# A score product on half of the array's rows becomes one on all 128, padded with zeros

## The chip, the cores and the metric

The kernel runs on one core of a Trainium2 chip. A core has a matrix engine (PE, with its weight loads shown apart as PEld), a vector engine (DVE), a scalar engine (ACT), a general engine (POOL) and queues that start transfers (SP). The metric is the time of one execution on the device, in microseconds (us); lower is better.

## The reference, cut to what matters

The program is one inference step of a backbone of two layers on 640 tokens: 128 of a prompt and 512 of an image. Each layer has a convolution, a gated recurrence and a differential attention side by side, then a feed-forward part. The change touches the attention alone:

```python
def one_block(qblk):                       # 128 queries
    s = einsum('bqhcd,bkhcd->bhcqk', qblk, k) * scale   # 4 heads, 2 maps c, 64 channels d
    p = softmax(s, axis=-1)
    w = p[:, :, 0] - lam * p[:, :, 1]
    return einsum('bhqk,bkhe->bqhe', w, v)
```

A head has 128 channels: 64 for its first map of scores and 64 for its second. The prompt attends to itself (128 keys). The 512 image queries attend to 640 keys: 128 of a cache and their own 512. Everything is float32.

## The kernel before, in words

**Exact products in parts.** The matrix engine gets its operands in a rounded 32-bit form (fp32r). A float32 factor is therefore kept as a high part and a low part, and a product is made of three: high by high, high by low, low by high. Nearly all large products of the kernel (L268 with channels on partitions, L279 with tokens on partitions) run over these three with all 128 rows, and an output takes 24 matmuls.

**Scores.** Since a map has only 64 channels, the parts share the 128 rows. `split_keys` (L948 to L955) makes, for each map `c` of a head, 128 rows of keys: the 64 rows of the map itself (`own`) hold the high parts, the 64 others (`other`) the low parts. `split_queries` (L957 to L964) makes three blocks of 128 columns for a tile of 128 queries: block 0 has the high parts of map 0 on both halves of the rows, block 1 those of map 1, and block 2 the low parts, map 0 on rows 0 to 63 and map 1 on rows 64 to 127. In `scores` (L973 to L1003) L987 multiplies block `c` by all 128 rows of keys, which gives high by high and high by low at once; L988 adds low by high, and takes only the 64 rows `rs` of the map:

```python
T.matmul(ps[:, hf, :320], lhsT=qs[n][:, c], rhs=ks[:, sl], start=True, stop=False)
T.matmul(ps[:, hf, :320], lhsT=qs[n][rs, 2], rhs=ks[rs, sl], start=False, stop=True)
```

This pair runs for two maps and for two halves of 320 keys, so a tile of queries takes eight matmuls, in turn on 128 and on 64 rows. There are four image tiles for each of four heads in two layers: 32 such tiles. A fifth tile of each head, the prompt's (L991), is made directly in float32 on 64 rows.

**A tile's way.** Behind the scores DVE takes the maximum over the keys (L994) and scales it (L995), and ACT makes the exponentials (L997). `weigh` (L1005) joins the two maps on DVE (L1007 to L1010), `turn` (L1013) transposes the weights on PE (L1016) and ACT copies them (L1017), `values` (L1020) multiplies them by the values (L1024). The weights of a tile are made one tile behind its scores. Two pairs of PSUM banks hold the scores of the two maps, so the next tile's scores need the exponentials of this one.

**What runs beside it.** `weave` puts one step of a list of large products behind each `yield` of the attention: products for gates (L268) beside heads 0 and 1 and the start of the recurrence (L279, then L268) beside heads 2 and 3. Their weights are split as they arrive by ACT (L249) and DVE (L250). `behind(last, taps, 4)` (L1002) puts four taps of the convolution (L639, DVE) behind the scaled maxima of each tile. The order on each engine is fixed when the program is built, by a planner that goes by priorities, dependencies and its own estimates of time; in the trace the first queries are split (L961 to L963) long before their scores.

**Storage.** `parts` (L1220) is a region of 3840 columns, taken anew in each layer. It holds the keys of two heads (2 times 1536 columns) and the queries of two tiles (2 times 384).

Of the kernel before, what the change touches and what calls it, by code (L numbers as in the profile page):

```python
# [15 lines left out]
ALU = mybir.AluOpType  # L16
AX = mybir.AxisListType

P = 128
# [5 lines left out]
# taps of the convolution beside the making of queries and keys, and beside a tile of scores  # L25
# [4 lines left out]
# columns of the parameter pack  # L30
# [5 lines left out]
# columns of the row pack (one layer)  # L36
# [3 lines left out]
class Arena:  # L40
    """Columns of one tile, given out and taken back in program order; the tile's
    own tracking orders the accesses. The part that has been free longest goes first."""
# [51 lines left out]
def tile_trunk_step(  # L94
# [33 lines left out]
    # ---------------------------------------------------------------- storage  # L128
# [41 lines left out]
    def banks(kind):  # L170
        """Banks for the large products; pairs for scores and levels; the rest."""
# [26 lines left out]
    # ---------------------------------------------------------------- helpers  # L198
# [12 lines left out]
    def flat(pair):  # L211
        """The first 640 columns of two banks."""
        return pair.rearrange("p b n -> p (b n)")[:, :NT]

    def f32(ap):
        return ap.bitcast(F32)
# [8 lines left out]
    def next_t():  # L225
        """For what is done with at once."""
        ctr["t"] += 1
        return ur[:, 3 + ctr["t"] % 2]

    def load_raw(src, n, at=None):  # L230
        """One panel of weights: n columns per partition."""
        if at is None:
            ctr["raw"] += 1
            at = rawt[:, ctr["raw"] % 2, :n]
        dst = at
        if len(src.shape) == 3:
            dst = at.rearrange("p (a b) -> p a b", a=src.shape[1])
        with hp():
            nc.sync.dma_start(dst, src)
        return at  # L240

    def split_cols(raw3):
        """Weights [128, K, c] into two parts that float32r holds exactly; list over k of (hi, lo)."""
# [16 lines left out]
    def gemm(wk, ak, hf):  # L260
        """sum_k w_k^T a_k for one half of the tokens; the three products that float32 holds."""
# [9 lines left out]
    def gemm_tm(wk, ak, i):  # L271
        """(token tile i of a)^T w; [128, 256]."""
# [9 lines left out]
    def panel8(src):  # L282
        """A panel [128, 8, 256]: two column tiles, each a list over k."""
        raw = load_raw(src, RAW).rearrange("p (k c) -> p k c", k=KD)
        return [split_cols(raw[:, :, c * P : (c + 1) * P]) for c in range(2)]
# [5 lines left out]
    def panel_wide(src, K):  # L291
        """A panel [128, K <= 4, 512]: four column tiles."""
# [8 lines left out]
    def rsqrt(dst, var, n):  # L301
        """dst = var ** -0.5 for var > 0."""
# [9 lines left out]
    def stat_rstd(s, sl, scale, eps, post=None, ring=None):  # L312
        """s: [128 ch, 640] whose column sums are the squares; 1 / rms of the tokens of sl
        on every partition, in a psum bank."""
# [15 lines left out]
    def streams(sl):  # L330
        """The parts of a slice of tokens that belong to the prompt (0) and to the latents (1)."""
# [6 lines left out]
    # ---------------------------------------------------------------- constants  # L338
# [16 lines left out]
    # ---------------------------------------------------------------- modulation  # L355
    def modulation(l, v, stage=None):
        """Vector v of the six of layer l: 1024 channels, both streams; channels on partitions.
        In steps of one panel."""
# [23 lines left out]
    def mod_finish(l, v, j=0, n=8):  # L382
        """n of the 8 tiles of channels of a vector, from j."""
# [10 lines left out]
    def mod_vectors(*regs):  # L394
        """The other vectors, the last of layer 0 first, on the vector engine, channels on
        partitions; in steps of one tile of channels."""
# [26 lines left out]
    def weave(core, fill, late=iter(())):  # L423
        """The steps of core with a step of fill behind each; the rest of fill before its end,
        with late."""
# [7 lines left out]
    def spread(fill, other):  # L433
        """The steps of fill, with one of other behind every third."""
# [9 lines left out]
    # ---------------------------------------------------------------- norm + modulation of the stream  # L444
# [19 lines left out]
    def make_h(xs, sq, l, which, hf):  # L464
        """h = rmsnorm(x) * (1 + scale) + shift, in two parts, for one half of the tokens."""
# [16 lines left out]
    # ---------------------------------------------------------------- layer parameters  # L482
    def layer_params(l):
        """Small vectors of a layer; 0 = -lambda, 1 = hgrn gain / 4, 2 = subln gain * (1 - lam_init),
        4..7 conv_b * 2, 8..11 ln_g / 2, 12..15 ln_b / 2."""
# [17 lines left out]
    def rope_tables(l):  # L503
        """Rotation tables with the gains in them: y = n * C + swap(n) * S."""
# [24 lines left out]
    def lower_bounds():  # L529
# [12 lines left out]
        for l in range(DEPTH):  # L542
            # rows: 0 = (1 - lb) / 2, 1 = lb + (1 - lb) / 2, 2 = -(1 - lb) / 2
# [10 lines left out]
    # ---------------------------------------------------------------- evictions  # L554
# [7 lines left out]
    def ev_silu2(dst):  # L562
        """2 silu(x) = (tanh(x / 2) + 1) x"""
# [8 lines left out]
    def tiles_g(jobs, lead=False):  # L572
        """jobs: (load, ((evict, k-list of activations), ...)); load() gives the column tiles of a
        panel. lead: the first two panels by halves, so that the second half may come later.
        In steps of half a column tile."""
# [21 lines left out]
    # ---------------------------------------------------------------- conv branch  # L597
# [32 lines left out]
    def conv_taps(l, pads, accs):  # L630
        """In steps of one tap."""
# [10 lines left out]
    def behind(ins, gen, n):  # L642
        """n steps of gen, not before ins on the vector engine."""
# [3 lines left out]
    def conv_norm(l, reg, accs):  # L647
        """Layer norm over 512 channels, in place; the accumulators hold twice the convolution.
        In steps of a few instructions."""
# [11 lines left out]
        for j in range(4):  # L661
            # in place: the prompt first, then the latents move down over the gap
# [15 lines left out]
    def conv_swish(l, reg, accs, out):  # L678
        """In steps of one tile."""
# [14 lines left out]
    # ---------------------------------------------------------------- HGRN  # L694
    def hgrn_v(l, out):
        """Values, tokens on partitions; [128, 5, 128] per head."""
# [10 lines left out]
    def hgrn_gemm(l, hb, h):  # L707
        """Queries (q), forget gates (f, b) and output gates (g) of a head; the last go to DRAM."""
# [10 lines left out]
    def both(rs, B=None):  # L719
        """Two regions as one, [128, 2, n]; with B: [128, blocks, 2, B], the first halves of the  # L720
        blocks of 2B from the first region and the second halves from the second."""
# [9 lines left out]
    def hgrn_core(l, h, vs, hb, bo):  # L731
        """Both directions of one head (b = backward, f = forward). q, k: [128 d, 2, 640]; chunks
        of 128 tokens, merged pairwise: at block length B the pairs (t, s) in the two halves of a
        block of 2B have the decay split at the middle, so that every factor is at most one. The
        first halves of the keys count forward and those of the queries backward, so one product
        holds both directions."""
# [63 lines left out]
        # states at chunk boundaries  # L800
# [57 lines left out]
    def token_norm(ot, scale, eps):  # L858
        """ot: [128 tok, 5, 128] in place / rms over the last axis."""
# [10 lines left out]
    # ---------------------------------------------------------------- attention  # L870
# [6 lines left out]
    def attn_qk(l, p, w, tabs):  # L877
        """Queries (w = 0) or keys (w = 1) of heads 2p, 2p+1: normed, rotated, transposed."""
# [18 lines left out]
        # prompt: gain only; latent: gain and rotation  # L897
# [23 lines left out]
    def attn_tr(l, p, w, reg, prep):  # L921
        """The queries or keys of attn_qk with the channels on partitions."""
        sq, s3, _ = prep
        # keys: 128 of the cache, 512 latents, 128 of the prompt; queries without the cache
# [22 lines left out]
    def split_keys(regs, parts, g):  # L947
        """Keys of head g on 128 rows for each of its two maps: (hi, lo) and (lo, hi)."""  # L948
        k = attn_views(regs[g // 2])[1][:, g % 2]
        ks = parts[:, g % 2 * 1536 : (g % 2 + 1) * 1536].rearrange("p (c t) -> p c t", c=2)  # L950
# [6 lines left out]
    def split_queries(q, dst):  # L957
        """A tile of queries as (hi, hi) of the first map, of the second, and (lo, lo) of both."""
        for c in range(2):
# [3 lines left out]
            V.tensor_tensor(out=dst[own, 2], in0=q[own], in1=f32(dst[own, c]), op=ALU.subtract)  # L963
        return dst  # L964

    def attn_core(l, p, regs, parts, keys, out, taps, ends):
        """Two heads; the weights of a tile of 128 queries are made one tile behind the scores.
        keys: the parts of the keys by head, made one head ahead; ends: what is left to do for
        the head before, and then for the last."""
# [5 lines left out]
        def scores(n, hh, i):  # L975
# [4 lines left out]
            for c in range(2):  # L980
                ps = wring.next()
                rs = slice(64 * c, 64 * (c + 1))
                if i:
                    ks = keys[2 * p + hh][:, c]
                    for hf in range(2):
                        sl = slice(hf * 320, (hf + 1) * 320)
                        T.matmul(ps[:, hf, :320], lhsT=qs[n][:, c], rhs=ks[:, sl], start=True, stop=False)  # L987
                        T.matmul(ps[:, hf, :320], lhsT=qs[n][rs, 2], rhs=ks[rs, sl], start=False, stop=True)  # L988
# [15 lines left out]
        def weigh(es, sm, nk):  # L1004
            # w' = e0 - lambda * (s0 / s1) * e1;  the weights are w' / s0  # L1005
# [37 lines left out]
        for n, it in enumerate(items + [None]):  # L1043
# [4 lines left out]
            if n + 1 < len(items) and items[n + 1][1]:  # L1048
                hh, i = items[n + 1]
                dst = parts[:, 3072 + n % 2 * 384 : 3456 + n % 2 * 384].rearrange("p (c t) -> p c t", c=3)  # L1050
                qs[n + 1] = split_queries(q3[:, hh, (i - 1) * P : i * P], dst)
# [18 lines left out]
    # ---------------------------------------------------------------- gates, branches, merge  # L1070
# [21 lines left out]
    def gates_out(l, b, js, dst):  # L1092
        """The tanh of half the gates of a branch, kept in DRAM."""
# [9 lines left out]
    def branch_g(l, b, ms, src, js, first=False, fin=None, gates=None):  # L1103
        """m_j (+)= (tanh(gate / 2) + 1) y"""
# [36 lines left out]
    def accumulate(load, ak, xs, g, other=iter(()), every=4):  # L1141
        """x_j += g_j * (w_j^T a), by halves of the tokens within a column tile; a step of other
# [312 lines left out]
```

## Time and profile before

| | |
|---|---|
| median of 3 runs | 2509.78 us (2509.27 to 2509.84) |
| span of the profiled execution, first to last instruction | 2509.0 us |
| granted clock of PE, mean over the span | 0.997 of full speed |
| PE busy, instructions | 2480.4 us, 17054 |
| DVE busy, instructions | 1747.9 us, 3570 |
| ACT busy, instructions | 916.8 us, 1741 |
| POOL busy, instructions | 2.6 us, 28 |

The profiled execution has no time of its own beside its span; the median of the runs stands 0.8 us above that span. A matmul's duration in the profile contains the time in which it overlaps its neighbours, so distances between starts tell the pace, not durations. Columns of the views are explained where their rows stand.

### The profile page before, as it was taken

How to read it: one execution, taken by the hardware profiler on the slowest of the kernel's cores; microseconds unless marked ns; L12 is line 12 of the kernel's file. 1: busy time of each engine (PE TensorE's matmuls, PEld its weight loads, DVE VectorE, ACT ScalarE, POOL GpSimd, SP SyncE). 2: the span in 40 equal slices, each digit the busy share in tenths (PEclk: the TensorE clock that was granted, in tenths of full speed). 3: DMA queues.
4: the chain of work that ended last, by engine and by line, in shares of the span. 5: the costliest groups of instructions: out<-in, count | busy, mean ns of one | idle time of the engine just before them, and what ended most of it. 6: DMA issues, size and time to landing. Idle time of an engine off the chain costs nothing.

```text
span 2509.0 us, 41312 instructions
## 1 busy us (share of the span) xinstructions
PE 2480.4 (99%) x17054; PEld 2393.0 (95%) x17054; DVE 1747.9 (70%) x3570; ACT 916.8 (37%) x1741; POOL 2.6 (0%) x28
## 2 busy tenths in 40 slices
PE   6999999999999999999999999999999999999999
PEld 4999889999999999999999998899999999999999
DVE  8587788685778897767685868885667884444343
ACT  5244565544332422222243445543433242222221
POOL 0000000000000000000000000000000000000000
PEclk8999999999999999999999999999999999999999
DMA  6222111432243354343332222012222412221221
GB/s 268 75 86 92 70 57 57 145 131 103 76 159 112 110 182 154 120 149 135 137 110 77 99 80 77 34 63 73 80 83 71 151 68 68 85 85 68 76 77 59
DMA packets 60492, 251.01 MB, mean 100 GB/s; under 512 B 6416, under 2 KB 18448, under 8 KB 37776
## 3 DMA queue, kind: packets, MB, share of 16 engines
q1 hardware_dynamic: 60304, 248.37, 28.5%
q8 instruction: 134, 2.20, 0.4%
q14 instruction: 54, 0.44, 0.1%
HBM read 230.52 MB, written 17.83 MB: 99 GB/s over the span
## 4 chain that ended last, share of the span: by engine, by line
PE 96%; DVE 2%; DMA 1%; ACT 1%; issue 0%; SPq 0%; DVEq 0%; ACTq 0%
PE psum L268 74%; PE psum L279 9%; PE psum L778 3%; PE psum L988 2%; PE psum L1024 2%; PE psum L987 1%; PE psum L369 1%; PE psum L1016 1%; PE psum L819 1%; DVE wR L250 1%; DMA aF<-in_wmod_dram 1%; PE psum L933 0%; PE psum L834 0%; PE psum L318 0%; PE psum L837 0%
## 5 line engine op out<-in xcount | busy, mean ns | idle before, releaser
L268 PE MATMUL psum<-hR,wR 128*128 128x256 f32 (+1 forms) x8832 | 1342.7, 311 | 3.1 <-ACT hR L478 2.1
L268 PEld LDWEIGHTS psum<-hR,wR 128*128 128x128 f32 x8832 | 1301.7, 190 | 10.9 <-issue 4.4
L250 DVE TENSOR_TENSOR wR<-rawt,wR 128x1024 fp32r<-128x1024 f32 x324 | 395.3, 1223 | 346.0 <-ACT wR L249 345.2
L249 ACT CAST wR<-rawt 128x1024 fp32r<-128x1024 f32 x324 | 338.4, 1047 | 785.6 <-PE psum L268 679.6
L268 PE MATMUL psum<-oR,wR 128*128 128x256 f32 (+1 forms) x4032 | 609.5, 310 | 0.3 <-DVE aF L1138 0.3
L268 PEld LDWEIGHTS psum<-oR,wR 128*128 128x128 f32 x4032 | 592.1, 189 | 3.3 <-DVE aF L1138 0.5
L1138 DVE SCALAR_TENSOR_TENSOR aF<-psum,modd,aF 128x128 f32<-128x128 f32 (+1 forms) x432 | 174.1, 435 | 105.0 <-PE psum L268 102.8
L279 PE MATMUL psum<-wR,hR 128*128 128x256 f32 x1920 | 243.0, 285 | 0.0
L279 PEld LDWEIGHTS psum<-wR,hR 128*128 128x128 f32 x1920 | 233.5, 191 | 3.5 <-issue 2.8
L639 DVE SCALAR_TENSOR_TENSOR aF<-aF,pk 128x655 f32<-128x655 f32 x240 | 214.9, 895 | 2.9
L411 DVE CUSTOM_DVE_ANT_0 aF<-aF 128x1024 f32<-128x1024 f32 x112 | 136.6, 1219 | 0.8
L1335 DVE TENSOR_TENSOR ur<-ur,psum 128x256 f32<-128x256 f32 (+1 forms) x88 | 42.9, 487 | 75.5 <-PE psum L268 75.5
L994 DVE TENSOR_REDUCE small<-psum 128x1 f32<-128x640 f32 (+1 forms) x80 | 56.6, 714 | 45.0 <-PE psum L988 41.0
L254 ACT CAST oR<-ur 128x256 fp32r<-128x256 f32 (+2 forms) x96 | 45.8, 479 | 93.9 <-DVE ur L1335 83.8
L778 PE MATMUL psum<-aF 128*128 128x128 f32 x560 | 78.1, 287 | 0.7 <-ACT aF L766 0.7
L778 PEld LDWEIGHTS psum<-aF 128*128 128x128 f32 x560 | 72.2, 191 | 4.3 <-ACT aF L766 1.6
L567 ACT ACTIVATE ur<-psum 128x256 f32<-128x256 f32 (+1 forms) x104 | 45.3, 436 | 72.3 <-PE psum L268 72.1
L766 ACT COPY aF<-aF 128x640 f32<-128x640 f32 x56 | 43.8, 782 | 72.8 <-DVE aF L782 59.6
L997 ACT ACTIVATE aF<-psum,small 128x640 f32<-128x640 f32 (+1 forms) x80 | 56.6, 711 | 25.8 <-DVE small L995 25.6
L255 DVE TENSOR_TENSOR oR<-ur,oR 128x256 fp32r<-128x256 f32 (+2 forms) x96 | 49.3, 515 | 19.7 <-ACT oR L254 19.7
L568 DVE SCALAR_TENSOR_TENSOR ur<-ur,psum 128x256 f32<-128x256 f32 (+1 forms) x104 | 50.2, 483 | 16.6 <-ACT ur L567 16.5
L369 PE MATMUL psum<-wR,cpad 128*8 128x512 f32 x160 | 46.4, 424 | 11.7 <-ACT wR L249 9.9
(170 smaller groups left out, 1761.6 us busy)
## 6 DMA issues: line engine op xcount, KB each, us to landing
rawt<-in_win_dram SPq DMA_DIRECT2D x64, 1024.0 KB, 4.8
rawt<-in_wfi_dram SPq DMA_DIRECT2D x44, 1024.0 KB, 4.7
aF<-in_wmodT_dram SPq DMA_DIRECT2D x28, 1024.0 KB, 4.8
rawt<-in_wfo_dram SPq DMA_DIRECT2D x20, 1024.0 KB, 4.9
rawt<-in_wmod_dram SPq DMA_DIRECT2D x12, 1024.0 KB, 4.8
rawt<-in_wbr_dram SPq DMA_DIRECT2D x24, 512.0 KB, 3.4
aF<-in_wmod_dram SPq DMA_DIRECT2D x8, 1024.0 KB, 10.5
aF<-in_xT_dram SPq DMA_DIRECT2D x16, 320.0 KB, 6.0
```

The lines of the kernel that those rows point to most:

```text
L249: S.copy(hi, raw3)
L250: V.tensor_tensor(out=lo, in0=raw3, in1=f32(hi), op=ALU.subtract)
L268: T.matmul(ps, lhsT=w, rhs=a[:, sl], start=k == 0 and q == 0, stop=k == n - 1 and q == 2)
L279: T.matmul(ps, lhsT=a[:, sl], rhs=w, start=k == 0 and q == 0, stop=k == n - 1 and q == 2)
L369: T.matmul(ps, lhsT=cpad[:, k, 4 - 4 * i : 12 - 4 * i], rhs=w, start=i == 0 and k == 0 and j == 0, stop=i == 1 and k == 7 and j == 1)
L411: V.tensor_tensor_reduce(out=out, in0=w[:, q * 1024 : (q + 1) * 1024], in1=cb[s], scale=1.0, scalar=0.0, op0=ALU.mult, op1=ALU.add, accum_ ...
L568: V.scalar_tensor_tensor(out=dst[:, sl], in0=dst[:, sl], scalar=1.0, in1=ps, op0=ALU.add, op1=ALU.mult)
L639: V.scalar_tensor_tensor(out=accs[j], in0=pads[j][:, t : t + CO], scalar=w(j, t), in1=accs[j], op0=ALU.mult, op1=ALU.add)
L778: T.matmul(ps[:, c // 4, (c % 4) * P : (c % 4 + 1) * P], lhsT=kc[:, c * P : (c + 1) * P], rhs=qm[:, c * nc1 : (c + 1) * nc1], start=True, ...
L994: V.tensor_reduce(out=mx[:, c : c + 1], in_=srcs[c], axis=AX.XY, op=ALU.max)
L997: S.activation(e.rearrange("p (h n) -> p h n", h=2 if i else 1), srcs[c], AF.Exp, bias=mx[:, c : c + 1], scale=0.125, accum_out=sm[:, c : ...
L1138: last = V.scalar_tensor_tensor(out=x[:, ss], in0=ps[:, ss.start - sl.start : ss.stop - sl.start], scalar=g[:, s : s + 1], in1=x[:, ss], o ...
```

## The change

The low parts of the queries get two blocks in place of one: block `2 + c` holds those of map `c` on its own 64 rows and zeros on the 64 others. L988 takes this block and the keys on all 128 rows; the low parts of the keys meet zeros. The zeros are written once per layer and buffer by POOL, four memsets of 64 rows by 128 columns, and the later splits leave them alone. A query buffer grows from 384 to 512 columns. To make room, the parts of the keys are made of the first 640 columns of a head (cache and image) and no longer of all 768; the last 128, the prompt's keys, were not used in this form. The rest of the diff takes away comments.

```diff
     def split_keys(regs, parts, g):
-        k = attn_views(regs[g // 2])[1][:, g % 2]
-        ks = parts[:, g % 2 * 1536 : (g % 2 + 1) * 1536].rearrange("p (c t) -> p c t", c=2)
+        k = attn_views(regs[g // 2])[1][:, g % 2, :NT]
+        ks = parts[:, g % 2 * 2 * NT : (g % 2 + 1) * 2 * NT].rearrange("p (c t) -> p c t", c=2)
...
     def split_queries(q, dst):
...
-            V.tensor_tensor(out=dst[own, 2], in0=q[own], in1=f32(dst[own, c]), op=ALU.subtract)
+            V.tensor_tensor(out=dst[own, 2 + c], in0=q[own], in1=f32(dst[own, c]), op=ALU.subtract)
         return dst
 
+    def query_parts(parts, n):
+        return parts[:, 4 * NT + n % 2 * 512 : 4 * NT + (n % 2 + 1) * 512].rearrange("p (c t) -> p c t", c=4)
...
                         T.matmul(ps[:, hf, :320], lhsT=qs[n][:, c], rhs=ks[:, sl], start=True, stop=False)
-                        T.matmul(ps[:, hf, :320], lhsT=qs[n][rs, 2], rhs=ks[rs, sl], start=False, stop=True)
+                        T.matmul(ps[:, hf, :320], lhsT=qs[n][:, 2 + c], rhs=ks[:, sl], start=False, stop=True)
...
-                dst = parts[:, 3072 + n % 2 * 384 : 3456 + n % 2 * 384].rearrange("p (c t) -> p c t", c=3)
-                qs[n + 1] = split_queries(q3[:, hh, (i - 1) * P : i * P], dst)
+                qs[n + 1] = split_queries(q3[:, hh, (i - 1) * P : i * P], query_parts(parts, n))
...
         parts = ao.alloc(6 * NT, -1)
+        for n in range(2):
+            for c in range(2):
+                G.memset(f32(query_parts(parts.ap, n)[64 * (1 - c) : 64 * (2 - c), 2 + c]), 0.0)
```

## Rows read from the trace of the kernel before

**Rows 1.** The page, parts 1 and 2: busy time, and tenths in 40 slices.
```profile
PE 2480.4 (99%) x17054; PEld 2393.0 (95%) x17054; DVE 1747.9 (70%) x3570; ACT 916.8 (37%) x1741; POOL 2.6 (0%) x28
PEclk8999999999999999999999999999999999999999
```

**Rows 2.** Windows, the two attention stretches: length, busy us by engine, clock, DMA share, GB/s.
```profile
228.00:425.00 197.00, 196.93 (x1268) 174.04 (x1267) 160.14 (x328) 110.46 (x279) 0.00 (x0) 1.00 0.18 63
1470.00:1667.00 197.00, 196.94 (x1263) 173.82 (x1262) 160.73 (x333) 110.43 (x276) 0.00 (x0) 1.00 0.17 59
```

**Rows 3.** The chain that ended last, within 228 to 425 us, by line.
```profile
by line: PE psum L268 46.9%; PE psum L279 15.0%; PE psum L988 11.0%; PE psum L1024 10.2%; PE psum L987 9.1%; PE psum L1016 4.5%; PE psum L991 0.8%; PE psum L1032 0.8%; PE psum L752 0.6%; ACT oR L953 0.4%; ACT aF L1017 0.4%; ACT aF L1027 0.2
```

**Rows 4.** Instructions of L987 and L988: count, shortest/median/longest ns, first and last start, shape.
```profile
L987 PEld LDWEIGHTS psum<-oR x128: 186/186/246, 228.6 to 1649.3; 128*128 128x128 f32 x128
L988 PEld LDWEIGHTS psum<-oR x128: 182/183/183, 229.0 to 1649.7; 64*128 64x128 f32 x128
```

**Rows 5.** Waits of PEld over the span: us in total, times, longest.
```profile
PEld psum L988 <- issue: 19.8, 126, 0.2
PEld psum L987 <- issue: 13.1, 84, 0.2
```

**Rows 6.** Timeline of one tile: start us, length, engine, line, shape, count, [idle before].
```profile
241.47 4.14 PEld L268 LDWEIGHTS psum<-hR,wR 128*128 128x128 f32 x24 [0.15 <-issue]
241.47 4.46 PE L268 MATMUL psum<-hR,wR 128*128 128x384 f32 x24
245.77 0.71 PE L1016 MATMUL psum<-ident,aF 128*128 128x128 f32 x5
246.23 3.12 PE L268 MATMUL psum<-hR,wR 128*128 128x256 f32 x24
249.19 1.27 PE L1024 MATMUL psum<-aF 128*128 128x128 f32 x10
250.22 0.39 PE L987 MATMUL psum<-oR 128*128 128x320 f32 x1
250.54 0.18 PEld L988 LDWEIGHTS psum<-oR 64*128 64x128 f32 x1 [0.16 <-issue]
250.54 0.41 PE L988 MATMUL psum<-oR 64*128 64x320 f32 x1
250.88 0.41 PE L987 MATMUL psum<-oR 128*128 128x320 f32 x1
251.22 0.41 PE L988 MATMUL psum<-oR 64*128 64x320 f32 x1
...
252.92 4.46 PE L268 MATMUL psum<-hR,wR 128*128 128x384 f32 x24
```

**Rows 7.** Timeline of PE where L991 (64 rows) alternates with L279 (128 rows).
```profile
319.90 0.48 PE L991 MATMUL psum<-aF 64*128 64x128 f32 x2
320.31 0.38 PE L279 MATMUL psum<-wR,hR 128*128 128x256 f32 x1
320.63 0.48 PE L991 MATMUL psum<-aF 64*128 64x128 f32 x2
```

**Rows 8.** Windows of the stretches beside L279 in layer 0, columns as in rows 2.
```profile
322.20:332.40 10.20, 10.20 (x73) 8.85 (x71) 6.44 (x18) 4.99 (x16) 0.00 (x0) 1.00 0.00 0
332.40:344.30 11.90, 11.90 (x87) 10.64 (x86) 10.59 (x26) 6.47 (x15) 0.00 (x0) 1.00 0.01 1
344.30:354.30 10.00, 10.00 (x72) 8.57 (x71) 9.87 (x18) 6.29 (x20) 0.00 (x0) 1.00 0.30 106
354.30:371.90 17.60, 17.60 (x135) 16.10 (x135) 15.62 (x32) 10.41 (x28) 0.00 (x0) 1.00 0.06 8
```

**Rows 9.** Waits of DVE from 322 to 372 us.
```profile
DVE small L1007 <- ACT aF L997: 4.3, 3, 3.1
DVE wR L250 <- ACT wR L249: 1.0, 2, 0.7
DVE small L864 <- ACT junk L862: 0.6, 1, 0.6
```

**Rows 10.** Timeline around the tile at 354 us: maximum, exponential, next scores.
```profile
351.32 0.82 DVE L994 TENSOR_REDUCE small<-psum 128x1 f32<-128x640 f32 x1
353.36 0.81 ACT L997 ACTIVATE aF<-psum,small 128x640 f32<-128x640 f32 x1
354.39 0.39 PE L987 MATMUL psum<-oR 128*128 128x320 f32 x1
```

**Rows 11.** First splits of queries in layers 0 and 1; the memsets of POOL.
```profile
L961 ACT CAST oR<-aF x4: 296/298/299, 136.1 to 138.6; 64x128 fp32r<-64x128 f32 x4
L961 ACT CAST oR<-aF x4: 297/299/302, 1377.4 to 1379.9; 64x128 fp32r<-64x128 f32 x4
L607 POOL MEMSET aF<- 128x15 f32 x24 | 2.4, 161 | 1302.8 <-DVE ur L477 1300.9 <-PE psum L268 0.8 <-DVE rs L306 0.7
```

## The prediction, made before the changed kernel ran

> **What bounds the kernel now.** I read the page first. It shows PE busy for 99% of the span and its granted clock at the upper level (2.4 GHz) in every slice but the first [rows 1]. So time is won where PE's stream gets shorter, unless another engine then falls behind. Next I cut out the two stretches in which scores are made, one per layer, with the windows: both are 197 us long, PE is busy throughout, DVE for 160 to 161 us, ACT for 110 us [rows 2]. The chain that ended last agrees: from 228 to 425 us it is PE nearly everywhere, with L987 and L988 together at 20.1% of the stretch (11.0 + 9.1), some 40 us, and only about 1% on ACT [rows 3]. That is a large share for 64 pairs of small products, and it made me look at the order in time.
>
> The timeline of one tile shows why [rows 6]. In a run of L268 matmuls on 128 rows the starts stand close: 24 of them with 384 columns take 241.47 to 245.77, that is 0.179 us each, and 24 with 256 columns take 246.23 to 249.19, 0.123 us each. The scores, with 320 columns, should lie between. But L987 and L988 follow each other at 0.34 us (250.54, 250.88, 251.22). Before nearly every one of them the weight load stood idle for 0.15 to 0.16 us with nothing that the profile can name ("issue"): 126 of the 128 loads of L988, and 84 of L987 [rows 5]. The neighbours differ in one thing from a run of L268: the rows in use change, 128, 64, 128, 64. The same is seen in a place that has nothing to do with fp32r: a single L279 matmul (256 columns) between two L991 products on 64 rows takes 0.32 us from its start to the next (320.31 to 320.63) where 0.123 is its pace in a run [rows 6, 7]. The excess is 0.20 us. So a change between 64 and 128 rows costs PE about 0.19 us, each way, in which neither load nor matmul starts.
>
> **The change part by part.**
>
> *The eight score matmuls of a tile.* Now all use 128 rows, so nothing changes within a tile or at its end. A tile takes 250.22 to 252.92 = 2.70 us now [rows 6]. Afterwards eight matmuls of 320 columns run at the pace of an unbroken run; 320 is halfway between 256 and 384, so (0.123 + 0.179) / 2 = 0.151 us, and a tile takes 8 x 0.151 = 1.21 us. Saved: 1.49 us. There are 128 / 4 = 32 tiles [rows 4], 32 x 1.49 = 47.7 us. It can be counted the other way: 128 L988, two changes each, 256 x (0.34 - 0.151) = 48.4 us. The bounds of the pace are its two neighbours: at 0.179 a tile saves 1.27 us and all 40.6; at 0.123 it saves 1.72 us and all 55. I take the middle. The zero half costs nothing by itself: the load of L987 on 128 rows takes 186 ns, that of L988 on 64 rows 183 ns [rows 4]. The prompt's tiles (L991) keep their changes.
>
> Two rules of the Trainium skill bear on this and disagree. "TensorEngine Tiling (Array Packing)", section "Key Properties", says that changing the tiling mode drains the engine; by it the saving is the one above, and the 0.34 and 0.32 us agree. "TensorE: Matmul & The Clock Gate", section "Part 3: Packing small matmuls — row/col tiling", says that a weight load overlaps running matmuls only when its row group differs. By it a load for all 128 rows would always wait, and 0.34 us would stay: the second rival below. The 24 loads of L268, all on the same rows, run within the time of their matmuls here (4.14 of 4.46 us), so the trace is against that rule.
>
> *Splits and memsets.* The splits of the queries are as many and as long as before. The splits of the keys get a sixth shorter; they lie on ACT and DVE beside PE, and I count nothing for them. The new work is eight memsets on POOL, four per layer. The trace has none of this shape; the nearest are POOL's memsets of 15 columns, 161 ns on average, and a DVE or ACT pass over 64x128, about 0.3 us [rows 11]. Between 0.1 and 1 us each, at most 4 us in a layer. What hides them: POOL is idle (2.6 us in the whole span [rows 1]), and the region is free when the first queries are split, at 136.1 and 1377.4 us [rows 11], while the first scores start at 228.6 [rows 4] and some 1470 us [rows 2]. If that cover were gone, PE would wait those 4 us per layer. I take 0. The first scores gain a wait on POOL; behind it on PE stands everything, but it is over some 90 us earlier.
>
> *What is late next.* A stretch of 197 us loses 16 x 1.49 = 24 us and becomes 173; DVE still has its 160 us in it [rows 2]. On the whole it fits, but not evenly. From 322.2 to 371.9, beside L279, four tiles are scored, and DVE is busy 6.44 + 10.59 + 9.87 + 15.62 = 42.5 of 49.7 us [rows 8]. Less 4 x 1.49 leaves 43.7 us for it. It is idle for 7.2 us there now. A wait of 3.1 us for an exponential [rows 9] is one of ACT behind PE, and shrinks with PE; the other 3 or so (1.2 of the same kind, 1.0 for weights cast by ACT, 0.6 for the norm) are delays of ACT itself and can stay. That makes 42.5 + 3 = 45.5 against 43.7 us: DVE comes some 2 us late. PE feels that soon, since at 354 us it has little in hand: the exponential that frees the bank of the first map ends at 353.36 + 0.81 = 354.17 and the next scores start at 354.39 [rows 10]. The bounds are 0 (taps slip behind what PE needs) and the whole gain of these tiles, 6 us a layer. I take 1.5 us a layer, 3 in all.
>
> *Sum.* 2509.0 - 47.7 + 3.0 = 2464.3 us of span; with the 0.8 us by which the median stands above the span, 2465.1. Predicted: 2465 us, its own range 2456 to 2475.
>
> **The rivals.**
>
> *DVE sets the pace beside L279 and around it.* For it: 9.87 of 10 us busy [rows 8]. Against it: half of DVE's idle time there is itself a wait on the PE chain. If eight tiles a layer gave back half of their gain, 2 x 8 x 0.75 = 12 us, the time is 2477; if they gave back all, 24 us, it is 2489. I price it at 2480.
>
> *The pace does not change.* If a load for rows that a running matmul uses always waited for that matmul, or if 0.34 us came from something else that L987 and L988 share (operands out of one region, two products into the same bank), the time stays 2510. For it: no two score matmuls on 128 rows follow each other anywhere in this trace. Against it: L991 and L279 show the same excess with other operands and other banks [rows 7], and the runs of L268 load the same rows 24 times, and put 24 products into one bank, without it [rows 6].
>
> *PE waits for the exponentials at every tile.* The planner builds the order anew. If it put a tile's scores straight behind the last tile's, without the runs of L268 or L279 between, PE would wait for the two maxima and exponentials of the tile before. From the end of the scores (252.92) to the second exponential it takes two maxima of 0.82 us, their scaling and two exponentials of 0.81 us [rows 10], at most about 3 us after the scores. All 32 tiles would lose 32 x 3 = 96 us, net 2558 us. It decides from 1.49 us of waiting per tile. For it: nothing but that the order is free within priorities. Against it: the kernel weaves a step of large products behind each step of the attention, and no instruction is added that would change their places.
>
> **How the numbers follow.** The forecast has 0.85. DVE as the pace 0.09, no change 0.04, slower 0.02. The range takes the forecast's own, 2456 to 2475 (from the upper bound of the saving, 55, less 2, to the lower, 40.6, with 6 lost), and goes up to 2479 for the milder half of the first rival. What a measurement can tell from no change is 0.2%, 5 us; the first two cases are beyond it on the fast side: 0.94 faster, 0.04 the same, 0.02 slower.
>
> **What would show it.** In the changed kernel's timeline L987 and L988 should follow each other at about 0.15 us, eight of them in 1.2 us, and the "issue" waits of their loads should be gone. L991 should keep its. The stretch from the first to the last scores should be 22 to 24 us shorter in each layer, and the rest of the span as long as before. A DVE that comes late would show as waits of L987 for ACT's L997, or of L279 for L250, between 320 and 390 us, with DVE near 97% busy. The memsets should stand on POOL long before the first scores. The prediction is wrong if the pace stays above 0.2 us, or if PE's waits in the two stretches grow by more than some 6 us a layer.

## The result, and the profile after

The changed kernel takes 2463.82 us (median, 2462.6 to 2463.97) against 2509.53 us for the kernel before on the same chip: a ratio of 0.9817, 95% interval 0.9803 to 0.9831. The forecast was 2465 us. The profiled execution's span is 2461.9 us, 47.1 us shorter than before. In the later runs the time of the profiled execution stands 2.1 to 2.2 us above its span, so the span of 2509.0 would belong to an execution of some 2511 us; for the whole, the 45.7 us between the medians are the better figure.

The page after, part 1. It is read against [rows 1]:

```profile
PE 2434.0 (99%) x17054; PEld 2384.4 (97%) x17054; DVE 1740.9 (71%) x3570; ACT 912.8 (37%) x1741; POOL 4.1 (0%) x36
```

PE issues as many instructions as before, 17054, and is busy for 46 us less. POOL has eight instructions more. Where the 47 us went is seen from the first weight load of the scores and the first of the recurrence (L752), in each layer. For the kernel after, the instructions of these two lines (count, shortest/median/longest ns, first and last start), layer 0 and then layer 1:

```profile
L992 PEld LDWEIGHTS psum<-oR x64: 186/188/192, 228.3 to 384.6; 128*128 128x128 f32 x64
L752 PEld LDWEIGHTS psum<-aF x40: 186/192/192, 398.6 to 658.8; 128*128 128x128 f32 x40
L992 PEld LDWEIGHTS psum<-oR x64: 186/188/192, 1446.2 to 1602.5; 128*128 128x128 f32 x64
L752 PEld LDWEIGHTS psum<-aF x40: 186/192/192, 1616.5 to 1853.2; 128*128 128x128 f32 x40
```

And for the kernel before, where the scores start at 228.6 [rows 4] and, in layer 1, at 1470.0:

```profile
L752 PEld LDWEIGHTS psum<-aF x40: 186/192/192, 422.2 to 682.3; 128*128 128x128 f32 x40
L752 PEld LDWEIGHTS psum<-aF x40: 186/192/192, 1663.7 to 1900.4; 128*128 128x128 f32 x40
```

The stretch from the first scores to the recurrence took 193.6 and 193.7 us and takes 170.3 and 170.3: 23.3 and 23.4 us less, together 46.7 of the 47.1. From the recurrence of layer 0 to the scores of layer 1 it was 1047.8 us and is 1047.6; from the recurrence of layer 1 to the end of the span 845.3 us and is 845.4. The rest of the span is as long as before to within 0.3 us.

Inside a stretch, the timeline of one tile after, to be read against [rows 6]:

```profile
245.78 1.27 PE L1029 MATMUL psum<-aF 128*128 128x128 f32 x10
246.81 0.39 PE L992 MATMUL psum<-oR 128*128 128x320 f32 x1
246.89 0.19 PEld L993 LDWEIGHTS psum<-oR 128*128 128x128 f32 x1
247.04 0.30 PE L993 MATMUL psum<-oR 128*128 128x320 f32 x1
247.04 0.19 PEld L992 LDWEIGHTS psum<-oR 128*128 128x128 f32 x1
247.19 0.31 PE L992 MATMUL psum<-oR 128*128 128x320 f32 x1
...
247.91 0.31 PE L993 MATMUL psum<-oR 128*128 128x320 f32 x1
247.91 4.18 PEld L268 LDWEIGHTS psum<-hR,wR 128*128 128x128 f32 x24
248.06 4.35 PE L268 MATMUL psum<-hR,wR 128*128 128x384 f32 x24
```

Behind the first one the matmuls now start 0.146 us apart (247.04 to 248.06 in seven steps), each load runs beside the matmul before it, and no "issue" idle stands before a load. Over the whole span the two kinds that led [rows 5] are gone from the waits of PEld. The tile takes 246.81 to 248.06, 1.25 us in place of 2.70, and the 24 matmuls of L268 behind it take 4.35 us in place of 4.46 [rows 6]. The prompt's products, still on 64 rows, keep their price; PE beside L279 after, against [rows 7]:

```profile
307.79 0.48 PE L996 MATMUL psum<-aF 64*128 64x128 f32 x2
308.20 0.38 PE L279 MATMUL psum<-wR,hR 128*128 128x256 f32 x1
308.52 0.48 PE L996 MATMUL psum<-aF 64*128 64x128 f32 x2
```

The single L279 still takes 0.32 us to the next start. And the memsets on POOL, in the timeline after:

```profile
0.73 0.96 POOL L1227 MEMSET oR<- 64x128 f32 x4 [0.29 <-POOLq L1442]
1246.60 0.20 POOL L1227 MEMSET oR<- 64x128 f32 x1 [1184.04 <-PE psum L268]
1264.16 0.70 POOL L1227 MEMSET oR<- 64x128 f32 x3 [17.36 <-PE psum L268]
```

They take about 0.2 us each and are done more than 180 us before the scores that read them.

### The profile page after: what moved, and what is told of

Same layout as the page of the kernel before. It is cut to its first block, busy times and chain, and to the rows that moved or that the text cites. A ratio compares the mean times of both kernels' runs of the same rounds, so it can differ in the third digit from the quotient of the medians.

```text
span 2461.9 us, 41318 instructions
## 1 busy us (share of the span) xinstructions
PE 2434.0 (99%) x17054; PEld 2384.4 (97%) x17054; DVE 1740.9 (71%) x3570; ACT 912.8 (37%) x1741; POOL 4.1 (0%) x36
## 4 chain that ended last, share of the span: by engine, by line
PE 95%; DVE 3%; ACT 1%; DMA 1%; issue 0%; SPq 0%; DVEq 0%; ACTq 0%
PE psum L268 74%; PE psum L279 9%; PE psum L778 3%; PE psum L1029 2%; PE psum L369 1%; PE psum L992 1%; PE psum L1021 1%; PE psum L993 1%; PE psum L819 1%; DVE wR L250 1%; DMA aF<-in_wmod_dram 1%; PE psum L933 0%; PE psum L834 0%; PE psum L318 0%; PE psum L837 0%
## 5 line engine op out<-in xcount | busy, mean ns | idle before, releaser
L268 PE MATMUL psum<-hR,wR 128*128 128x256 f32 (+1 forms) x8832 | 1340.3, 310 | 3.2 <-ACT hR L478 2.1
L268 PEld LDWEIGHTS psum<-hR,wR 128*128 128x128 f32 x8832 | 1302.6, 190 | 7.4 <-ACT hR L478 2.5
L250 DVE TENSOR_TENSOR wR<-rawt,wR 128x1024 fp32r<-128x1024 f32 x324 | 395.1, 1222 | 340.3 <-ACT wR L249 339.7
L268 PE MATMUL psum<-oR,wR 128*128 128x256 f32 (+1 forms) x4032 | 609.5, 310 | 0.3 <-DVE aF L1142 0.3
L268 PEld LDWEIGHTS psum<-oR,wR 128*128 128x128 f32 x4032 | 592.1, 189 | 3.3 <-DVE aF L1142 0.5
L279 PE MATMUL psum<-wR,hR 128*128 128x256 f32 x1920 | 240.7, 284 | 0.0
L279 PEld LDWEIGHTS psum<-wR,hR 128*128 128x128 f32 x1920 | 234.1, 192 | 0.7
L567 ACT ACTIVATE ur<-psum 128x256 f32<-128x256 f32 (+1 forms) x104 | 45.3, 435 | 72.6 <-PE psum L268 72.2
L1002 ACT ACTIVATE aF<-psum,small 128x640 f32<-128x640 f32 (+1 forms) x80 | 56.5, 710 | 23.4 <-DVE small L1000 23.1
L558 ACT ACTIVATE ur<-psum 128x256 f32<-128x256 f32 (+1 forms) x80 | 34.4, 434 | 62.6 <-PE psum L268 62.6
```

What stands on the lines that cost most here:

```text
L250: V.tensor_tensor(out=lo, in0=raw3, in1=f32(hi), op=ALU.subtract)
L268: T.matmul(ps, lhsT=w, rhs=a[:, sl], start=k == 0 and q == 0, stop=k == n - 1 and q == 2)
L279: T.matmul(ps, lhsT=a[:, sl], rhs=w, start=k == 0 and q == 0, stop=k == n - 1 and q == 2)
L1002: S.activation(e.rearrange("p (h n) -> p h n", h=2 if i else 1), srcs[c], AF.Exp, bias=mx[:, c : c + 1], scale=0.125, accum_out=sm[:, c : ...
```

## The experiments

The theory is that PE pays about 0.19 us for each change between matmuls on 64 and on 128 rows, and for nothing else. The rivals: the gain comes from what else the change does (separate blocks, shorter key splits, a new order); a product on 64 rows is slow by itself; a load waits for running matmuls on its rows. Counted along PE's order in the traces, the kernel before has 280 changes of rows in its two stretches, the changed one 24, all of them at the prompt's tiles.

**Half the rows, all else as changed.**

```diff
-T.matmul(ps[:, hf, :320], lhsT=qs[n][:, 2 + c], rhs=ks[:, sl], start=False, stop=True)
+T.matmul(ps[:, hf, :320], lhsT=qs[n][rs, 2 + c], rhs=ks[rs, sl], start=False, stop=True)
```

> The changed kernel with its memsets, its separate blocks for the low parts and its shorter splits of the keys, but with the low product on the 64 rows of its map again (the zeros are not read). Theory (each change between 64 and 128 rows costs PE 0.19 us): the gain goes, 2509.5 us, L992 and L993 0.34 us apart. Rival (the gain came from the separate blocks, the shorter splits or the new order): 2464 us, 0.147 us apart.

Measured: 2509.56 us, before 2509.67, ratio 1.000 (0.9991 to 1.001). PE in the timeline of this run:

```profile
249.09 0.41 PE L993 MATMUL psum<-oR 64*128 64x320 f32 x1
249.43 0.41 PE L992 MATMUL psum<-oR 128*128 128x320 f32 x1
249.77 0.41 PE L993 MATMUL psum<-oR 64*128 64x320 f32 x1
```

The starts are 0.34 us apart again. Blocks, memsets and shorter splits are worth nothing that can be measured (the interval is 0.1% wide on either side, 2.5 us); the gain is in the rows of this one product.

**The kernel before, grouped by map.** First both halves of the keys on 128 rows, then both on 64:

```diff
 for hf in range(2):
     sl = slice(hf * 320, (hf + 1) * 320)
     T.matmul(ps[:, hf, :320], lhsT=qs[n][:, c], rhs=ks[:, sl], start=True, stop=False)
+for hf in range(2):
+    sl = slice(hf * 320, (hf + 1) * 320)
     T.matmul(ps[:, hf, :320], lhsT=qs[n][rs, 2], rhs=ks[rs, sl], start=False, stop=True)
```

> The kernel before, its low products still on 64 rows, but for each map first both products on 128 rows (the two halves of the keys) and then both on 64 rows: four changes of rows per tile in place of eight. Theory (a price per change): 32 tiles x 4 x 0.19 = 24 us less, 2485 us; inside a pair 0.147 us, at each change 0.34 us. Rival (a product on 64 rows is slow by itself, or a load waits for running matmuls that use its rows): 2509.5 us, 0.34 us everywhere.

Measured: 2485.17 us, ratio 0.9903 (0.9888 to 0.9918). PE in its timeline:

```profile
247.84 0.54 PE L987 MATMUL psum<-oR 128*128 128x320 f32 x2
248.30 0.56 PE L990 MATMUL psum<-oR 64*128 64x320 f32 x2
248.79 0.56 PE L987 MATMUL psum<-oR 128*128 128x320 f32 x2
249.28 0.56 PE L990 MATMUL psum<-oR 64*128 64x320 f32 x2
249.77 1.49 PE L268 MATMUL psum<-hR,wR 128*128 128x384 f32 x7
```

The loads of a pair in the same run and, in narrower windows, matmuls one by one:

```profile
248.30 0.29 PEld L990 LDWEIGHTS psum<-oR 64*128 64x128 f32 x2 [0.19 <-issue]
248.07 0.30 PE L987 MATMUL psum<-oR 128*128 128x320 f32 x1
248.30 0.41 PE L990 MATMUL psum<-oR 64*128 64x320 f32 x1
248.56 0.30 PE L990 MATMUL psum<-oR 64*128 64x320 f32 x1
```

A pair takes 0.49 us, 0.20 more than two intervals of 0.146. The loads stand idle 0.19 us before the first of a pair and not before the second. But the starts are not 0.15 and 0.34 us apart, as was expected: they are 0.23 apart across the change (248.07 to 248.30) and 0.26 behind it (to 248.56). About half of the price shows in the interval behind the change. The same 64-row products, on the same operands, cost half as much extra when there are half as many changes, and a pair on 128 rows takes as long as a pair on 64. That excludes the product being slow by itself. The trace has 156 changes; 24.5 us less for 124 fewer is 0.198 us each.

**One map on 128 rows.**

```diff
-T.matmul(ps[:, hf, :320], lhsT=qs[n][:, 2 + c], rhs=ks[:, sl], start=False, stop=True)
+w = slice(0, P) if c == 0 else rs
+T.matmul(ps[:, hf, :320], lhsT=qs[n][w, 2 + c], rhs=ks[w, sl], start=False, stop=True)
```

> The changed kernel with the low product of map 0 on 128 rows and that of map 1 on its 64 rows: four changes of rows per tile. Theory: half of the gain, 2509.5 - 23 = 2486 us. Rival (any 64-row product in a tile sets a slower mode for the tile, or the gain has another source): 2509.5 or 2464 us.

Measured: 2484.28 us, ratio 0.9900 (0.9883 to 0.9916). 152 changes; 25.4 us for 128 fewer, again 0.198 us each. Two different ways to halve the changes give the same time within 1 us, and neither time of the rival, 2509.5 or 2464, came.

**The kernel before, grouped by tile.** Four products on 128 rows, then four on 64, the maps in turn:

```diff
 T.matmul(ps[:, hf, :320], lhsT=qs[n][:, c], rhs=ks[:, sl], start=True, stop=False)
-T.matmul(ps[:, hf, :320], lhsT=qs[n][rs, 2], rhs=ks[rs, sl], start=False, stop=True)
...
+if i:
+    for hf in range(2):
+        for c in range(2):
...
+            T.matmul(srcs[c][:, hf], lhsT=qs[n][rs, 2], rhs=keys[2 * p + hh][rs, c, sl], start=False, stop=True)
```

> The kernel before with the four products of a tile on 128 rows first, then its four on 64 rows, those of map 0 (rows 0 to 63) and map 1 (rows 64 to 127) in turn: two changes of rows per tile. Theory (a price per change): 32 x 6 x 0.19 = 36 us less, 2473 us. If in addition two products on different rows run side by side, two of the four cost nothing more: 32 x 2 x 0.147 = 9 us, 2464 us, and the four on 64 rows take 0.3 us together and not 0.6. Rival (64 rows are slow by themselves): 2509.5 us. What the maxima lose by starting later, about 0.4 us a tile, should lie beside the products of the gates.

Measured: 2469.54 us, ratio 0.9842 (0.9827 to 0.9856), between the two numbers expected. PE in its timeline:

```profile
254.66 1.27 PE L1029 MATMUL psum<-aF 128*128 128x128 f32 x10
255.69 0.82 PE L987 MATMUL psum<-oR 128*128 128x320 f32 x4
256.44 0.56 PE L997 MATMUL psum<-oR 64*128 64x320 f32 x4
256.93 2.35 PE L268 MATMUL psum<-hR,wR 128*128 128x384 f32 x12
```

In a window that begins later, the last two products of the tile and the whole run of L268 behind them:

```profile
256.69 0.31 PE L997 MATMUL psum<-oR 64*128 64x320 f32 x2
256.93 4.44 PE L268 MATMUL psum<-hR,wR 128*128 128x384 f32 x24
```

Four products on 64 rows take 0.49 us, as long as two on the same 64 rows took in the run grouped by map, and the last two lie within 0.31 us together, where one alone took 0.30 (248.56 above). So products on the upper and on the lower rows do run side by side. This tile takes 255.69 to 256.93, 1.24 us, as short as the changed kernel's. Yet the whole is 5.7 us slower. The trace shows two reasons. Beside heads 2 and 3 the planner pulls a tile's products apart, and there are 108 changes where two per tile and the prompt's would make 88; 20 x 0.19 is 3.8 us. And part of the price of a tile's last change falls behind the tile: the 24 matmuls of L268 take 4.44 us, in the changed kernel 4.35; 32 x 0.09 is 2.9 us. As estimates the two together are somewhat more than the 5.7 measured.

**No low product at all** (the low parts of the queries are left out of the scores).

> The changed kernel without the low product (the part of the scores from the low parts of the queries is left out; splits and memsets stay). It prices the padded product by itself. Theory (128 matmuls at 0.147 us on PE's path): 18.8 us less than the changed kernel, 2445 us; if DVE or ACT already set the pace beside heads 2 and 3, a quarter to a half of that is not seen there, 2450 to 2454 us. Rival (the zero half makes the product nearly free, or costs more than its pace): below 5 us, or above 25 us.

Measured: 2448.01 us, ratio to before 0.9757 (0.9742 to 0.9771). Against the changed kernel, over the kernels before of the two sets (2509.33 and 2509.53), that is 15.6 us less, where the bare price of 128 matmuls would be 18.8. The waits of PEld from 225 to 425 us in this run:

```profile
PEld psum L992 <- ACT aF L1001: 1.3, 5, 0.4
PEld psum L1028 <- ACT aF L1021: 0.8, 4, 0.3
```

and in the changed kernel:

```profile
PEld psum L1029 <- ACT aF L1022: 1.2, 6, 0.3
PEld psum L1037 <- DVE aF L868: 0.7, 3, 0.3
PEld psum L1021 <- ACT aF L1032: 0.4, 1, 0.4
PEld psum L992 <- ACT aF L1002: 0.2, 1, 0.2
```

The padded product costs no more than its pace. With it gone, the loads of the scores begin to wait for exponentials: 1.3 us in place of 0.2 in the first layer's stretch (the same in the second), which would make some 2 us of the 3 missing. The order of this run also has 28 changes of rows where the changed kernel has 24; four more are 0.8 us.

**No taps beside heads 2 and 3.** The taps beyond the first 80 of a layer are not issued:

```diff
+if j * 30 + t <= 80:
     V.scalar_tensor_tensor(out=accs[j], in0=pads[j][:, t : t + CO], scalar=w(j, t), in1=accs[j], ...)
```

> The changed kernel without the 40 taps of the convolution that stand on DVE beside heads 2 and 3 of each layer (the convolution is left incomplete): DVE has 36 us less in each stretch of scores. Theory A (the 1.7 us that are missing from the full gain are DVE coming late): the stretch from the first scores to the recurrence gets 0.5 to 1 us shorter in each layer, the whole about 2462 us. Theory B (they are short waits of PE for ACT's copies of the transposed weights): no change of the stretch, 2464 us. What DVE does after the stretch may start earlier in both.

Measured: 2463.81 us, the changed kernel's 2463.82; ratio to before 0.9819 (0.9802 to 0.9835). The window beside L279 in the changed kernel (length, busy us of PE, PEld, DVE, ACT, POOL, clock, DMA share, GB/s):

```profile
310.30:350.00 39.70, 39.70 (x322) 38.78 (x321) 38.74 (x89) 25.50 (x71) 0.00 (x0) 1.00 0.08 27
```

and nearly the same one without the taps:

```profile
310.00:350.00 40.00, 39.44 (x325) 38.78 (x325) 27.40 (x74) 26.28 (x75) 0.00 (x0) 1.00 0.08 27
```

DVE falls from 98% to 69% busy there and the kernel is not faster. But the run does not decide between the theories. Without the taps the planner made another order, and in it PEld waits longer for the norm at a head's end; from 225 to 425 us:

```profile
PEld psum L1038 <- DVE aF L869: 2.0, 4, 0.8
PEld psum L1030 <- ACT aF L1023: 1.1, 5, 0.3
```

In the changed kernel the same two waits are 0.7 and 1.2 us (L1037 and L1029 above). The 1.3 us more for the norm exceed the 0.5 to 1 us that theory A would give back, so they could hide it. What is shown is that DVE's busy share alone does not set the time; neither theory is shown.

## Why the prediction was right, point by point

**What bounds.** Right: the time was in PE's stream, in the intervals between L987 and L988, and the rest of the span did not move.

**The price of a change of rows.** Right in mechanism, and now shown three ways: undone alone it gives all the gain back; halved in two ways it gives somewhat more than half (24.5 and 25.4 of 45.7 us); and the price per change in the two halved runs, 0.198 us, is the 0.19 to 0.20 read from [rows 6] and [rows 7]. Over all 256 changes it comes to less, 45.7 / 256 = 0.18 us; where the rest may have gone stands below. One detail was wrong: the prediction has neither load nor matmul start within those 0.19 us, and the run grouped by map shows about half of the price behind the first matmul on the new rows. "TensorEngine Tiling (Array Packing)", section "Key Properties", of the Trainium skill says that changing the tiling mode drains the engine. The runs agree with it in that every change has a price; that the price is a drain they do not show. The rule weighed against it, from "TensorE: Matmul & The Clock Gate", section "Part 3: Packing small matmuls — row/col tiling" of the Trainium skill, is not what this trace shows: loads for all 128 rows start beside matmuls on the same rows (247.04 above).

**The size per tile.** Forecast 1.49 us saved, measured 2.70 - 1.25 = 1.45. The pace in a run is 0.146, a little better than the 0.151 taken halfway between the neighbours. But the first interval of a tile stays at 0.23 us (246.81 to 247.04), where the tile follows the float32 products of L1029. The sum took eight equal intervals; one of them also holds what the neighbour before leaves. What the sum left out is the run of L268 behind the tile, which gets 0.11 us shorter (4.46 to 4.35): with it the tile shown saves 1.56 us, which is eight changes at 0.195. Counted by changes, 256 x (0.34 - 0.146) = 49.7 us, an estimate, where the sum had 47.7. Of these, 45.7 us arrived in the medians and 47.1 in the spans, so 2.6 to 4.0 us are missing.

**DVE late beside L279.** The size was about right, the wait was not. DVE did fill up, as reckoned (98% of the window beside L279, 97% forecast). But the waits that the prediction named are hardly there: the loads of the scores waited for exponentials for 0.2 us a layer, and those of L279 for L250 not at all. Others grew. The waits of PEld from 225 to 425 us before, without the "issue" ones:

```profile
PEld psum L1024 <- ACT aF L1017: 0.8, 4, 0.3
PEld psum L1016 <- DVE small L995: 0.2, 1, 0.2
PEld psum L268 <- ACT aF L558: 0.2, 1, 0.2
PEld psum L987 <- ACT aF L1027: 0.2, 1, 0.2
```

That is 1.4 us. In the changed kernel the four lines shown with the run without the low product make 2.5, and with the same 0.2 us of L268 2.7 us: 1.2 for ACT's copies of the transposed weights, 0.7 for the norm at a head's end on DVE, 0.4 for ACT's scaled outputs (L1032). The growth is 1.3 us here and 1.1 in the stretch of the second layer (1.6 to 2.7), near the 1.5 a layer forecast. It is idle time of the loads and not the loss of PE itself, but the 2.4 us of both layers would nearly fill the gap to the spans. So the step from "DVE is full" to "PE waits for exponentials or for the weights of L279" did not hold, and DVE has only part of the growth. Why what little was in hand at one tile [rows 10] did not matter at the others is not shown; the order was made anew. The total fell within 1.3 us of the sum partly by luck: 2 us too little were reckoned as saved, and a loss of about the size forecast came from other waits.

**The memsets.** Right: 0.2 us each, inside the bounds of 0.1 and 1 us, and hidden.

**The rivals.** No change in the pace: out. DVE as the pace: out for this kernel, since at most 4 us are missing, where it had 12 to 24. PE waiting at every tile: not seen in the changed kernel, though its beginning shows when the low product is left out.

## What to carry to other kernels

When small matmuls cost far more than their columns, look at the rows in use of neighbours in PE's order, not at their durations: an "issue" idle of 0.15 to 0.2 us before a weight load at each turn from 64 to 128 rows and back was the sign here. Padding the smaller operand with zeros written once, or grouping by rows, removes the changes; padding is the safer of the two where a planner may pull a group apart. A second engine at 98% is a reason to look at which of its results the first engine awaits, not yet a loss.

## What was not expected

The expectation left open whether products on different rows run side by side. Products on rows 0 to 63 and on rows 64 to 127, issued in turn into different banks, overlapped almost fully: four took 0.49 us up to the next start on 128 rows, as long as two on the same rows. Grouped by tile, half-empty products therefore made a tile nearly as short as full ones (1.24 and 1.25 us, with 0.09 us more behind it), without memsets or larger buffers. That kernel stayed 5.7 us behind, by estimate through the 0.09 us of each tile and through the planner's order. That the price of a change shows in two intervals, 0.09 us in the one across the change and 0.11 in the one behind it where 0.146 is the pace, was not expected at all: the 0.34 us between neighbours in [rows 6] hold half of one change and half of the one before.
